# Attention values accumulated in the spare columns of the transposes' PSUM banks

## The chip, the cores and the metric

The kernel runs on one NeuronCore of a Trainium2 chip, as one launch. The metric is the device time of that launch in microseconds (us). Every execution computes the same outputs from the same inputs; before the change, three timed executions have a median of 949.86 us, between 949.14 and 950.73.

## The reference, cut to what matters

One encoder layer is applied to two sequences, a prompt of 256 tokens and a sample of 2048 tokens (2304 in all), of width 1024, in float32:

```
h = rms_norm(x, g_pre);  proj = h @ w_in            # 1024 -> 6 x 512
q, k, v, z_a, u_f, z_f = split(proj)
y_a = neighbourhood_attention(q, k, v, rpb)          # 8 heads of 64
y_f = fourier_mix(u_f) @ w_f + b_f
mixed = concat(rms_norm(y_a, g_na) * silu(z_a), rms_norm(y_f, g_f) * silu(z_f))
out = x + rms_norm(mixed @ w_out, g_post)
```

The tokens lie on a grid 64 columns wide (4 rows for the prompt, 32 for the sample). A query attends to 8 rows by 16 columns around it. The reference works on blocks of 16 query columns against a slab of 32 key columns, with a bias and a mask, a softmax, and a product with the values.

## The kernel before, in words

The projections and the Fourier half come first. The change lies in the third stage, which the code writes from line 1358 on: the attention itself, interleaved with the output projection of the Fourier half.

**Groups and steps.** The attention is cut into 36 groups: 4 pairs of heads (pr) by 9 groups. Group 0 of a pair (R is None) is the prompt; the other eight are 4 pairs of row blocks (R) by 2 halves of the columns (hc). Each group has two column blocks, b = 0 and 1, and two heads, h = 0 and 1. The loop at line 1554 runs k from 2 to 37; in step k it finishes group k-2 (called f) and starts group k (called g). The order of instructions on each engine is the order of the code (a manual schedule).

**One step, in the order of TensorE.** transp (line 1467) transposes the softmax weights of f, in pieces of 64 queries, into four PSUM banks ptb[0] to ptb[3]: block b and half y go to ptb[2b+y], alternating between y = 0 and y = 1. A bank holds 512 float32 columns; the transposes fill at most 384 of them. Each bank is then copied to SBUF (pt): the y = 0 banks by ScalarE (ACT), the y = 1 banks by VectorE (DVE), but in odd steps (the argument called short) block 1's y = 1 bank by ACT too. scores (line 1157) computes q times k of group g into four other banks. In even steps f_mm (line 1431) follows, twice: the projection of one tile of 128 tokens of the Fourier half, 12 matmuls into ptb[0] and 12 into ptb[1], each 512 columns wide, which f_evac (line 1441) scales into SBUF, the first by DVE, the second by ACT. Last comes pv (line 1485): the transposed weights times the values, for both blocks into one PSUM tile of 2 x 128 columns. That tile takes a bank of tag "c" in even steps and one of tag "a" in odd steps, the tags from which scores takes its banks.

**Gating.** The tile pv is read twice: DVE multiplies it with the gate za into y (line 1513), and ACT squares it (line 1515 for the first pair of heads, line 1519 for the others) for the later norm; GpSimd (POOL) adds the squares up (line 1520). y goes to HBM by SyncE's queue (lines 1524 and 1527). For the prompt's groups the multiplication, and the first pair's square, are split by block; for the others one instruction covers 256 columns.

**The other work of a step.** DVE adds the bias and takes the maximum for each of four score tiles (bias_max, line 1190), ACT exponentiates (exps, line 1202), DVE and POOL normalise (soft, line 1206). In even steps POOL, ACT and DVE also prepare the next tile of the Fourier half (lines 1396 to 1416). The last loop (line 1715) projects the attention half and uses ptb[0] and ptb[1] for a copy of g_post (line 1733).

**PSUM.** Of eight banks four are ptb[0] to ptb[3], three have tag "a", one tag "c". Waits between engines are generated by the framework from the order of the code and from which tiles an instruction reads or writes.

Of the kernel before, what the change touches and what calls it, by code (L numbers as in the profile page):

```python
# [10 lines left out]
F32 = mybir.dt.float32  # L11
F32R = mybir.dt.float32r
AF = mybir.ActivationFunctionType
ALU = mybir.AluOpType
# [165 lines left out]
def build(tc, A, O):  # L180
    nc = tc.nc
# [1176 lines left out]
    pt = ExitStack()  # L1358
# [59 lines left out]
    def out_mm(d, n, js, p, w):  # L1418
        for j in js:
            c, x = divmod(j, 3)  # L1420
            nc.tensor.matmul(p, (d["l"] if x == 2 else d["h"])[:, c], w(n, int(x == 1), c), start=j == 0, stop=j == 11)  # L1421
# [7 lines left out]
        nc.sync.dma_start(d["xt"], A["xn"][d["t"] * 128:d["t"] * 128 + 128, :])  # L1429

    def f_mm(d, n):
        d["p", n] = ptb[n]
        out_mm(d, n, range(12), ptb[n], lambda n, x, c: wo1[n][c][:, x])

    def a_mm(d, n):
        x = n or d is atiles[0]
# [27 lines left out]
        n = len(ds)  # L1464
        rsq_ops(inva[:, ds[0]["i"]:ds[0]["i"] + n], p[:, :n], n, 1.0 / 512)

    def transp(g, short):
        g["pt"] = []
        for b, ch in enumerate(g["ch"]):
            m = len(ch)  # L1470
            z = ch[0][0][1]
            o = jp.tile([128, 2, 384], F32, tag="pt", name="pt", bufs=PB)
            for j, c in enumerate(ch):
                for h in range(2):
                    for y, (c0, nk) in enumerate(c):
                        ys, x = slice(64 * y, 64 * y + 64), 64 * (h * m + j)
                        nc.tensor.transpose(ptb[2 * b + y][:nk, x:x + 64], g["w"][b][ys, h, c0:c0 + nk], ident[ys, ys])  # L1477
            ov = o.rearrange("p h (j y x) -> p y h j x", y=2, x=64)
            for y, copy in ((0, nc.scalar.copy), (1, nc.scalar.copy if b and short else V.tensor_copy)):
                copy(ov[:z, y, :, :m], ptb[2 * b + y][:z, :128 * m].rearrange("p (h j x) -> p h j x", h=2, x=64))  # L1480
            g["pt"].append(o)

    yt = {}

    def pv(g, short):
        pr, R = g["pr"], g["R"]
        p = ps.tile([128, 2, 128], F32, tag="a" if short else "c", name="pv", bufs=3 if short else 1)
        for b, pp in enumerate(g["pp"]):
            for j, y, nk, v, x, first, last in pp:
                o = slice(0, 128) if y is None else slice(64 * y, 64 * y + 64)  # L1490
                for h in range(2):
                    hs = slice(64 * h, 64 * h + 64)
                    nc.tensor.matmul(p[hs, b, o], v[:nk, b, x, hs], g["pt"][b][:nk, h, j * 128 + o.start:j * 128 + o.stop],  # L1493
                                     start=first, stop=last)
        ts = g["ts"]
        if R is None:
            hc = 0
            za = g["za"].rearrange("p (b r x c) -> p b x r c", b=2, x=2, c=16)
            view = lambda a: a.rearrange("p (r b x c) -> p b x r c", b=2, x=2, c=16)
            cut = lambda a: a.rearrange("p b (x r c) -> p b x r c", x=2, c=16)  # L1500
            cuts = lambda a: [a[:, b] for b in range(2)]
        else:
            cuts = lambda a: [a]
            hc = g["hc"]
            za = g["za"].rearrange("p (r b c) -> p b r c", b=2, c=16)
            view = lambda a: a.rearrange("p (r x b c) -> p x b r c", x=2, b=2, c=16)[:, hc]
            cut = lambda a: a.rearrange("p b (r c) -> p b r c", c=16)
        p4 = cut(p)
        both = lambda f, *a: [f(*x) for x in zip(*(cuts(y) for y in a))]
        if hc == 0:  # L1510
            yt[0] = jp.tile([128, 512], F32, tag="y", name="y", bufs=YB)
        y = yt[0][:, :ts.stop - ts.start]
        both(lambda o, i, z: V.tensor_tensor(out=o, in0=i, in1=z, op=ALU.mult), view(y), p4, za)
        if pr == 0:
            both(lambda o, i: nc.scalar.activation(o, i, AF.Square), view(ysq[:, ts]), p4)
        else:
            sq = jp.tile([128, 256], F32, tag="sqa", name="sqa", bufs=2)
            s4 = cut(sq.rearrange("p (b x) -> p b x", b=2))
            nc.scalar.activation(sq, p.rearrange("p b x -> p (b x)"), AF.Square)
            both(lambda o, i: nc.gpsimd.tensor_tensor(out=o, in0=o, in1=i, op=ALU.add), view(ysq[:, ts]), s4)  # L1520
        if R is None or hc:
            if R == 0:
                for x, r in enumerate(HALF[0]):
                    nc.sync.dma_start(yD[0, pr, :, TP + 64 * r:TP + 64 * r + 256], y[:, 256 * x:256 * x + 256])
            else:
                t0 = 0 if R is None else TP + 64 * HALF[R][0]
                nc.sync.dma_start(yD[0, pr, :, t0:t0 + y.shape[1]], y)
# [26 lines left out]
    for k in range(2, len(G) + 2):  # L1554
        pr, i = divmod(k, 9)
        g, p, f = G[k] if k < len(G) else None, G[k - 1] if k <= len(G) else None, G[k - 2]
        if pr < 3:
            if i == 3:
                load_k(pr + 1)
            if i == 5:  # L1560
                load_t(pr + 1, 0)
        if 0 < pr < 4 and i == 0:
            load_t(pr, 1)
        if k == 9:
            nc.sync.dma_start(gpb, pbc(A["gpost"]))
        if k == 23:
            wp = pt.enter_context(tc.tile_pool(name="wp", bufs=1, side="right"))
            WO.extend(wp.tile([128, 4, D], F32R, name="w0%d" % x) for x in range(2))
        if 24 <= k < 32:
            y = k - 24  # L1570
            nc.sync.dma_start(WO[y % 2][:, y // 2].bitcast(F32), woD[0, y % 2, y // 2])
        x = k // 2
        transp(f, k % 2)
        if k % 2:
            if g:
                scores(g)
                for b in range(2):
                    for h in range(2):
                        bias_max(g, b, h)
                        if b == 0:  # L1580
                            exps(g, b, h)
            else:
                a_mm(atiles[0], 1)
        else:
            if k > 2:
                soft(p, 0)
                exps(p, 1, 0)
                exps(p, 1, 1)
            if g:
                scores(g)  # L1590
                bias_max(g, 0, 0)
                exps(g, 0, 0)
                bias_max(g, 0, 1)
                exps(g, 0, 1)
                soft(p, 1)
                for h in range(2):
                    bias_max(g, 1, h)
                    exps(g, 1, h)
                if x < 17:
                    ys_mul(ftiles[x + 1])  # L1600
                if x < 16:
                    ys_load(ftiles[x + 2])
                f_mm(ftiles[x], 0)
            else:
                soft(p, 1)
                a_mm(atiles[0], 0)
            if k in NT:
                f_norm(NT[k])
            if k in (32, 34, 36):
                a_norm(atiles[{32: slice(6), 34: slice(6, 10), 36: slice(10, 14)}[k]])  # L1610
            if g:
                f_mm(ftiles[x], 1)
                soft(g, 0)
            run_later()
            if g:
                f_evac(ftiles[x], 0)
                soft(g, 1)
            for v, x0, x1 in YSQ.get(k, []):
                nc.scalar.activation(v[:, x0:x1], v[:, x0:x1], AF.Square)
                V.tensor_tensor(out=sqs[:, x0:x1], in0=sqs[:, x0:x1], in1=v[:, x0:x1], op=ALU.add)  # L1620
            if x < 17:
                ys_split(ftiles[x + 1])
            elif x == 17:
                ys_split(atiles[0])
            if g:
                f_evac(ftiles[x], 1)
        if pr < 3 and i == 7:
            mask_p(pr + 1)
        pv(f, k % 2)
        if k == 12:  # L1630
            pq_.close()
        if k + 1 < len(G):
            prep_v(G[k + 1])
        if k + 4 < len(G):
            prep(G[k + 4])
        if k == 28:
            xk = [kp.tile([128, T], F32, tag=x, name="xk", bufs=n) for x, n in (("kh", 2), ("kl", 1))]
        if 32 <= k < 36:
            x, d = k - 32, atiles[k - 32]
            d["xt"] = xk[x // 2][:, x % 2 * D:x % 2 * D + D]  # L1640
            nc.sync.dma_start(d["xt"], A["xn"][d["t"] * 128:d["t"] * 128 + 128, :])
        if k == 32:
            ys_load(atiles[0])
        if k in (34, 35):
            ys_load(atiles[k - 33])
            of_load(atiles[k - 34])
        if k == 36:
            ys_split(atiles[1])
# [114 lines left out]
```

## Time and profile before

| | |
|---|---|
| median of three timed executions | 949.86 us (949.14 to 950.73) |
| the profiled execution's own time | 948.03 us |
| its span, first to last instruction | 946.2 us |
| TensorE (PE) busy | 932.9 us, 99% of the span |
| DVE / ACT / POOL busy | 662.3 / 472.7 / 338.4 us |
| granted TensorE clock | 0.999 of full speed |
| the third stage, 617 to 846 us | PE 225.34, DVE 139.68, ACT 144.29, POOL 119.66 us busy of 229 |

PE is the row of matmuls and PEld that of the weight loads, which overlap matmuls. A row of the timeline gives the start in us, the duration, the engine, the line of the kernel, the operation, output and inputs, and how many were merged; brackets give how long the engine sat idle before it, and what ended that wait. In a list of waits, the three numbers are us in total, how often, and the longest.

### The profile page before, as it was taken

The page shows a single profiled execution, that of the slowest core. Times are in us where ns is not written, and L with a number is a line of the kernel's source. Part 1 is how long each engine was busy: PE and PEld are TensorE (multiplying, and loading weights), DVE is VectorE, ACT ScalarE, POOL GpSimd, SP SyncE. Part 2 cuts the span into 40 slices and gives each one's busy share as a digit, 9 for nine tenths or more (in the row PEclk, how much of TensorE's full clock was granted, in tenths as well). Part 3 has the DMA queues.
Part 4 walks back from the last instruction along what each step waited for, and adds up shares of the span by engine and source line. Part 5 has one row for each costly group of instructions (what it writes and reads, how often), then busy time and mean ns, then how long its engine had stood idle before and what let it go on. Part 6 is the DMA issues. An engine that isn't in the chain of part 4 may idle for free.

```text
span 946.2 us, 18823 instructions
## 1 busy us (share of the span) xinstructions
PE 932.9 (99%) x6800; PEld 779.8 (82%) x6800; DVE 662.3 (70%) x1287; ACT 472.7 (50%) x1053; POOL 338.4 (36%) x338
## 2 busy tenths in 40 slices
PE   9999999999999999999999999999999999999996
PEld 7889988888888888888888897978777787888885
DVE  6387987677875976696667454677565655649997
ACT  5846676532323642333344234567665666654443
POOL 3201202435650300453343000455455665524444
PEclk9999999999999999999999999999999999999999
DMA  9899776568665998669979789688788899879993
GB/s 335 319 373 372 219 281 253 164 229 312 222 266 191 363 410 322 259 217 315 326 266 325 260 312 324 222 271 240 243 271 242 259 286 272 266 238 365 339 339 126
DMA packets 146845, 265.20 MB, mean 280 GB/s; under 512 B 21888, under 2 KB 86784, under 8 KB 143872
## 3 DMA queue, kind: packets, MB, share of 16 engines
q1 hardware_dynamic: 146608, 263.99, 80.3%
q8 instruction: 54, 0.88, 0.4%
q14 instruction: 39, 0.32, 0.1%
q10 hardware_dynamic: 144, 0.00, 0.0%
HBM read 175.40 MB, written 95.88 MB: 287 GB/s over the span
## 4 chain that ended last, share of the span: by engine, by line
PE 95%; DVE 1%; DMA 1%; issue 1%; ACT 1%; POOL 0%; SPq 0%; DVEq 0%; POOLq 0%; ACTq 0%
PE mm L176 18%; PE mm L177 18%; PE mm L175 18%; PE ptb L1421 10%; PE po L1421 10%; PE pv L1493 5%; PE s L1177 4%; PE ptb L1477 3%; PE pab L1015 2%; PE py L175 1%; PE py L177 1%; PE py L176 1%; DMA rv<-wv 0%; DMA yz<-zD 0%; PE ppq L1052 0%
## 5 line engine op out<-in xcount | busy, mean ns | idle before, releaser
L175 PE MATMUL mm<-xh,wa 128*128 128x512 f32 x448 | 174.4, 389 | 0.0
L176 PE MATMUL mm<-xl,wa 128*128 128x512 f32 x448 | 174.3, 389 | 0.0
L177 PE MATMUL mm<-xh,wa 128*128 128x512 f32 x448 | 174.3, 389 | 0.0
L175 PEld LDWEIGHTS mm<-xh,wa 128*128 128x128 f32 x448 | 84.1, 188 | 17.5
L177 PEld LDWEIGHTS mm<-xh,wa 128*128 128x128 f32 x448 | 84.1, 188 | 17.5
L176 PEld LDWEIGHTS mm<-xl,wa 128*128 128x128 f32 x448 | 84.1, 188 | 17.3
L552 POOL TENSOR_TENSOR ws<-wr 128x512 f32<-128x512 f32 x16 | 22.2, 1389 | 185.1 <-DMA wr<-wz 167.6
L1421 PE MATMUL ptb<-wo,yh 128*128 128x512 f32 x272 | 86.8, 400 | 0.0
L1211 POOL TENSOR_SCALAR w<-w,m 128x352 f32<-128x352 f32 (+4 forms) x136 | 75.1, 566 | 32.8 <-DVE m L1208 17.7
L1421 PE MATMUL po<-w,yh 128*128 128x512 f32 x280 | 86.6, 391 | 0.0
L567 DVE TENSOR_TENSOR wa<-wr,wa 128x512 fp32r<-128x512 f32 x60 | 55.2, 926 | 33.3 <-ACT wa L566 33.2
L1204 ACT ACTIVATE w<-w,m 128x352 f32<-128x352 f32 (+4 forms) x136 | 69.9, 523 | 3.0 <-DVE m L1199 2.7
L869 DVE TENSOR_TENSOR f<-u,mm 128x512 f32<-128x512 f32 x64 | 43.6, 682 | 32.9 <-PE mm L177 28.0
L176 PE MATMUL mm<-vl,xh 128*128 128x512 f32 x168 | 65.5, 390 | 0.2 <-DVE vl L498 0.2
L175 PE MATMUL mm<-vh,xh 128*128 128x512 f32 x168 | 65.4, 389 | 0.0
L177 PE MATMUL mm<-vh,xl 128*128 128x512 f32 x168 | 65.4, 389 | 0.0
L1421 PEld LDWEIGHTS ptb<-wo,yh 128*128 128x128 f32 x272 | 49.3, 188 | 14.9 <-ACT pt L1480 4.1
L1421 PEld LDWEIGHTS po<-w,yh 128*128 128x128 f32 x280 | 52.3, 188 | 10.9
L1493 PEld LDWEIGHTS pv<-pt,v 96*64 96x64 f32 (+2 forms) x1280 | 45.7, 137 | 15.3 <-ACT pt L1480 8.9
L566 ACT CAST wa<-wr 128x512 fp32r<-128x512 f32 x60 | 36.4, 618 | 41.3 <-PE mm L177 17.0
L1199 DVE CUSTOM_DVE_ANT_1 w<-s,tb 128x264 f32<-128x264 f32 (+3 forms) x124 | 50.7, 455 | 7.0 <-PE s L1177 5.8
L1421 PE MATMUL po<-w,yl 128*128 128x512 f32 x140 | 54.5, 389 | 0.0
(246 smaller groups left out, 2171.6 us busy)
## 6 DMA issues: line engine op xcount, KB each, us to landing
wr<-wz SPq DMA_DIRECT2D x48, 512.0 KB
vl<-sD SPq DMA_DIRECT2D x20, 512.0 KB
xm<-xm SPq DMA_DIRECT2D x9, 1024.0 KB
oD<-ofs SPq DMA_DIRECT2D x18, 512.0 KB
of<-oD SPq DMA_DIRECT2D x18, 512.0 KB
yr<-yD SPq DMA_DIRECT2D x34, 256.0 KB
zD<-f SPq DMA_DIRECT2D x16, 512.0 KB
woD<-wo SPq DMA_DIRECT2D x16, 512.0 KB
```

The costliest lines, as they stand in the source:

```text
L175: nc.tensor.matmul(out, lh, rh, start=first, stop=False)
L176: nc.tensor.matmul(out, lh, rl, start=False, stop=False)
L177: nc.tensor.matmul(out, ll, rh, start=False, stop=last)
L566: nc.scalar.copy(o[:, 0], src)
L567: nc.vector.tensor_tensor(out=o[:, 1], in0=src, in1=o[:, 0].bitcast(F32), op=ALU.subtract)
L869: nc.vector.tensor_tensor(out=dst(f, b), in0=src(uu[u]), in1=src(p), op=op)
L1177: nc.tensor.matmul(sp[2 * b + h][64 * y:64 * y + 64, j * w:(j + n) * w], g["q"][hs, 128 * b + 64 * y:128 * b + 64 * y + 64], kk[hs, k:k + ...
L1199: nc.vector.tensor_tensor_reduce(out=rows(g["w"][b][:, h, :n], w), in0=rows(g["s"][2 * b + h][:, :n], w), in1=tv, scale=1.0, scalar=3.0e38 ...
L1204: nc.scalar.activation(w, w, AF.Exp, bias=m[:, h:h + 1], scale=-1.0, accum_out=m[:, 2 + h:3 + h])
L1211: nc.gpsimd.tensor_scalar(w, w, m[:, 4 + h:5 + h], 1.0, ALU.mult, ALU.mult)
L1421: nc.tensor.matmul(p, (d["l"] if x == 2 else d["h"])[:, c], w(n, int(x == 1), c), start=j == 0, stop=j == 11)
L1493: nc.tensor.matmul(p[hs, b, o], v[:nk, b, x, hs], g["pt"][b][:nk, h, j * 128 + o.start:j * 128 + o.stop], start=first, stop=last)
```

## The change

The values of block b are accumulated in columns 384 to 511 of ptb[b], the bank that also takes block 0's transposes of half y = b, instead of in a tile of their own. The projection of the Fourier half goes into ptb[2] and ptb[3], except for its first tile, which is computed before these two exist. The multiplication and the square are made per block for all groups, and read the two banks. The copy that ACT took in odd steps goes to DVE, as in even steps.

```diff
     def f_mm(d, n):
-        d["p", n] = ptb[n]
-        out_mm(d, n, range(12), ptb[n], lambda n, x, c: wo1[n][c][:, x])
+        p = d["p", n] = ptb[n if d is ftiles[0] else 2 + n]
+        out_mm(d, n, range(12), p, lambda n, x, c: wo1[n][c][:, x])
...
-    def transp(g, short):
+    def transp(g):
...
-            for y, copy in ((0, nc.scalar.copy), (1, nc.scalar.copy if b and short else V.tensor_copy)):
+            for y, copy in ((0, nc.scalar.copy), (1, V.tensor_copy)):
...
-    def pv(g, short):
+    def pv(g):
         pr, R = g["pr"], g["R"]
-        p = ps.tile([128, 2, 128], F32, tag="a" if short else "c", name="pv", bufs=3 if short else 1)
+        p = [ptb[b][:, 384:512] for b in range(2)]
...
-                    nc.tensor.matmul(p[hs, b, o], v[:nk, b, x, hs], g["pt"][b][:nk, h, j * 128 + o.start:j * 128 + o.stop],
+                    nc.tensor.matmul(p[b][hs, o], v[:nk, b, x, hs], g["pt"][b][:nk, h, j * 128 + o.start:j * 128 + o.stop],
                                      start=first, stop=last)
...
+        p = [cut(a) for a in p]
...
-        both(lambda o, i, z: V.tensor_tensor(out=o, in0=i, in1=z, op=ALU.mult), view(y), p4, za)
+        for b in range(2):
+            V.tensor_tensor(out=view(y)[:, b], in0=p[b], in1=za[:, b], op=ALU.mult)
         if pr == 0:
-            both(lambda o, i: nc.scalar.activation(o, i, AF.Square), view(ysq[:, ts]), p4)
+            for b in range(2):
+                nc.scalar.activation(view(ysq[:, ts])[:, b], p[b], AF.Square)
         else:
...
-            nc.scalar.activation(sq, p.rearrange("p b x -> p (b x)"), AF.Square)
-            both(lambda o, i: nc.gpsimd.tensor_tensor(out=o, in0=o, in1=i, op=ALU.add), view(ysq[:, ts]), s4)
+            for b in range(2):
+                nc.scalar.activation(cut(sq[:, b]), p[b], AF.Square)
...
```

The additions on POOL keep their number.

More of the change, by code (lines that the diff above doesn't have):

```diff
@@ L1499, in pv @@
             view = lambda a: a.rearrange("p (r b x c) -> p b x r c", b=2, x=2, c=16)
-            cut = lambda a: a.rearrange("p b (x r c) -> p b x r c", x=2, c=16)
-            cuts = lambda a: [a[:, b] for b in range(2)]
         else:
-            cuts = lambda a: [a]
             hc = g["hc"]
@@ L1506, in pv @@
             view = lambda a: a.rearrange("p (r x b c) -> p x b r c", x=2, b=2, c=16)[:, hc]
-            cut = lambda a: a.rearrange("p b (r c) -> p b r c", c=16)
-        p4 = cut(p)
-        both = lambda f, *a: [f(*x) for x in zip(*(cuts(y) for y in a))]
+        cut = lambda a: a.rearrange("p (x r c) -> p x r c", x=2, c=16) if R is None else \
+            a.rearrange("p (r c) -> p r c", c=16)
+        p = [cut(a) for a in p]
         if hc == 0:
@@ L1512, in pv @@
         y = yt[0][:, :ts.stop - ts.start]
-        both(lambda o, i, z: V.tensor_tensor(out=o, in0=i, in1=z, op=ALU.mult), view(y), p4, za)
+        for b in range(2):
+            V.tensor_tensor(out=view(y)[:, b], in0=p[b], in1=za[:, b], op=ALU.mult)
         if pr == 0:
-            both(lambda o, i: nc.scalar.activation(o, i, AF.Square), view(ysq[:, ts]), p4)
-        else:
-            sq = jp.tile([128, 256], F32, tag="sqa", name="sqa", bufs=2)
-            s4 = cut(sq.rearrange("p (b x) -> p b x", b=2))
-            nc.scalar.activation(sq, p.rearrange("p b x -> p (b x)"), AF.Square)
-            both(lambda o, i: nc.gpsimd.tensor_tensor(out=o, in0=o, in1=i, op=ALU.add), view(ysq[:, ts]), s4)
+            for b in range(2):
+                nc.scalar.activation(view(ysq[:, ts])[:, b], p[b], AF.Square)
+        else:
+            sq = jp.tile([128, 256], F32, tag="sqa", name="sqa", bufs=2).rearrange("p (b x) -> p b x", b=2)
+            for b in range(2):
+                nc.scalar.activation(cut(sq[:, b]), p[b], AF.Square)
+            o = view(ysq[:, ts])
+            if R is None:
+                for b in range(2):
+                    nc.gpsimd.tensor_tensor(out=o[:, b], in0=o[:, b], in1=cut(sq[:, b]), op=ALU.add)
+            else:
+                nc.gpsimd.tensor_tensor(out=o, in0=o, in1=sq.rearrange("p b (r c) -> p b r c", c=16), op=ALU.add)
         if R is None or hc:
@@ L1572, in build @@
         x = k // 2
-        transp(f, k % 2)
+        transp(f)
         if k % 2:
@@ L1628, in build @@
             mask_p(pr + 1)
-        pv(f, k % 2)
+        pv(f)
         if k == 12:
```

## The prediction

> **What bounds the kernel now.** I read the page first: the busy times, then the chain that ended last. Then one stretch, 617 to 846 us, which holds all steps of the changed loop, with its granted clock.
>
> ```profile
> span 946.2 us, 18823 instructions
> PE 932.9 (99%) x6800; PEld 779.8 (82%) x6800; DVE 662.3 (70%) x1287; ACT 472.7 (50%) x1053; POOL 338.4 (36%) x338
> PE 95%; DVE 1%; DMA 1%; issue 1%; ACT 1%; POOL 0%; SPq 0%; DVEq 0%; POOLq 0%; ACTq 0%
> 617.00:846.00 229.00, 225.34 (x3252) 182.84 (x3252) 139.68 (x510) 144.29 (x458) 119.66 (x187) 1.00 0.84 256
> ```
>
> PE sets the time, in the loop too: it idles 229.00 - 225.34 = 3.7 us there, while DVE, ACT and POOL are busy for little over half. So work added to DVE or ACT costs nothing by itself, and only what makes PE wait counts. The chain in order of time shows how PE runs through the end of an even step, an odd step, and into the next:
>
> ```profile
> 750.77 1.08 PE pv L1493 x32
> 751.85 0.83 PE ptb L1477 x23
> 752.68 1.21 PE s L1177 x20
> 753.89 0.07 issue
> 753.96 1.59 PE pv L1493 x40
> 755.55 0.84 PE ptb L1477 x22
> 756.39 0.73 PE s L1177 x7
> ```
>
> The reader should see that the next step's transposes (L1477) follow the values (pv, L1493) with nothing between them. Today they write other banks than pv does. After the change the first transposes write ptb[0] and ptb[1], the two banks that hold the values which DVE and ACT have yet to read. So the question is whether a transpose may start while they read other columns of its bank. The waits that the framework has put into this program answer most of it:
>
> ```profile
> ACT sqa L1519 <- DVE y L1513: 27.5, 24, 3.3
> DVE ds L1369 <- ACT dl L1367: 19.7, 9, 2.8
> ...
> 624.82 0.69 PE L1493 MATMUL pv<-pt,v 128*64 128x64 f32 x16
> 625.80 0.54 PEld L1477 LDWEIGHTS ptb<-ident,sc 64*96 64x96 f32 x15 [0.24 <-ACT ofs L1448]
> 626.12 0.48 DVE L1513 TENSOR_TENSOR y<-pv,za 128x128 f32<-128x128 f32 x2
> 626.69 0.45 ACT L1515 ACTIVATE ysq<-pv 128x128 f32<-128x128 f32 x2 [0.94 <-DVE y L1513]
> 627.19 0.37 PEld L1177 LDWEIGHTS s<-kk,q 64*64 64x64 f32 x10 [0.15 <-ACT ysq L1515]
> ```
>
> The square (L1519) takes nothing from the product y (L1513): both only read pv. Still ACT waits for DVE. The same holds for L1369, which reads the sum that L1367 read. So two engines are kept from reading one bank together. The rows at 626 show more: the prompt's group is already gated by block. Its two products run 626.12 to 626.60; the squares start at 626.69, after the second product, though the first square reads only the columns of the first product, done by about 626.40. That is the order of a whole bank, not of columns. One such pair is all that the trace has, and no row shows a PE write that waits for a reader of other columns.
>
> A rule of the Trainium skill bears on just that: the page PSUM — Partial Sum Buffer, section "PSUM bank collisions raise a hardware error", says that two of TensorE, ScalarE and VectorE on one bank and the same 32 partitions collide even on disjoint columns, reads against reads too, and that a program has to guard by bank. It speaks against this change. By it the sum is the one below; by column order it is the second rival. No run here shows a collision; the rows above agree with the guarding.
>
> **The change part by part.** First what the wait costs, from the step at 702.88:
>
> ```profile
> 702.88 0.91 PE L1477 MATMUL ptb<-ident,w 64*128 64x64 f32 x24
> 703.00 0.42 DVE L1513 TENSOR_TENSOR y<-pv,za 128x256 f32<-128x256 f32 x1 [2.63 <-PE pv L1493]
> 703.46 0.38 ACT L1519 ACTIVATE sqa<-pv 128x256 f32<-128x256 f32 x1 [1.30 <-DVE y L1513]
> 703.59 0.56 DVE L1480 COPY pt<-ptb 128x384 f32<-128x384 f32 x1 [0.16 <-PE ptb L1477]
> 703.73 1.28 PE L1177 MATMUL s<-kk,q 64*64 64x352 f32 x24
> 704.63 0.53 DVE L1199 CUSTOM_DVE_ANT_1 w<-s,tb 128x352 f32<-128x352 f32 x1 [0.49 <-PE s L1177]
> 705.31 1.59 PE L1493 MATMUL pv<-pt,v 128*64 128x128 f32 x40 [0.31 <-DVE m L1199]
> 706.23 0.08 DVE L1199 DVE_READ_ACCUMULATOR2_ANT m<- 128x1 f32 x1
> 706.84 0.90 PE L1477 MATMUL ptb<-ident,w 64*96 64x64 f32 x24
> ...
> L1513 DVE TENSOR_TENSOR y<-pv,za x40: 276/424/425, 626.1 to 844.5; 128x256 f32<-128x256 f32 x32, 128x128 f32<-128x128 f32 x8
> L1515 ACT ACTIVATE ysq<-pv x10: 272/383/384, 626.7 to 678.9; 128x256 f32<-128x256 f32 x8, 128x128 f32<-128x128 f32 x2
> ```
>
> *The new stall at each step's start.* pv computes block 0 first, in half of its 1.59 us, so block 0's product and square run under block 1's matmuls and the first transpose, into ptb[0], goes on time. The second, into ptb[1], must wait for block 1's square, and all later PE work queues behind it. Block 1's product can start when y starts now, 703.00; a 128x128 product takes 0.276 us (the minimum in its row), so 703.28; the hand-over to ACT takes 0.04 (703.42 to 703.46); a 128x128 square 0.272: 703.59; the hand-over to PE 0.05 (the squares end at 626.69 + 0.45 = 627.14, PEld starts at 627.19): 703.64. Today that second transpose starts one pace after the first: 0.91 / 24 = 0.04, so 702.92. The stall is 0.72 us. Transposes follow pv in steps 3 to 37, 35 times: 18 odd, 17 even.
>
> *After an odd step* DVE has more ahead of the product: it takes over ACT's copy. The copies start 0.72 later than 703.59, at 704.31, and two of 0.56 end at 705.43. The four bias passes, 704.63 to 706.31 today (1.68), then end at 707.11. PE's scores end at 703.73 + 1.28 + 0.72 = 705.73, and pv ends at about 705.8 + 1.59 = 707.39. Block 0's product fits between, and block 1's is not late: again 0.72, with 0.1 to 0.2 us of margin. Without that cover the stall grows by what DVE is late; one more copy, 0.56, bounds it. Sum: 35 x 0.72 = 25.2 us. Bounds: the bare product and square, 0.55 x 35 = 19.2, and 25.2 + 17 x 0.56 = 34.7.
>
> In the first step (k = 2) DVE is late already: the product starts at 626.12, when pv has ended at 624.82 + 0.69 = 625.51. There the stall is longer by that 0.6; the 0.24 that the transposes wait there now for ACT's projection read goes, since that read moves to ptb[3]. Net +0.4.
>
> *What is removed.* In odd steps pv waits after the scores, for its bank (DVE m L1199, freed by the first bias pass) and for the three copies in a row on ACT:
>
> ```profile
> PEld pv L1493 <- ACT pt L1480: 8.9, 17, 0.7
> ...
> 707.68 0.84 ACT L1480 COPY pt<-ptb 96x384 f32<-96x384 f32 x2
> 708.88 0.74 PE L1421 MATMUL ptb<-wo,yh 128*128 128x512 f32 x2
> ```
>
> At 753.89 this costs 0.07 idle and 0.07 in a pv that starts without preloaded weights (1.59, against 1.52 in even steps); at 705.01 (where the scores of 703.73 end) 0.30 and 0.07. After the change the last copy ends at 705.43, before the scores at 705.73, and the bank is long free. So 18 x 0.14 to 18 x 0.37: 2.5 to 6.7 us. I take 0.2 each, 3.6, nearer to the low end since the whole loop's idle PE time is only 3.7 us; the 8.9 us of idle weight loads lie mostly under matmuls.
>
> *The projection* in ptb[2] waits for ACT's second copy instead of its first. At 707.68 both copies together end at 708.52, PE reaches the projection at 708.88, and all of this moves by the same 0.72: cost 0. Without that margin it would be up to one copy, 17 x 0.42 = 7.1; a gain is excluded, as PE does not idle there. The reads of ptb[2] and ptb[3] end during pv, and block 1's transposes come half a transpose group later than block 0's: 0.
>
> *Smaller pieces.* DVE gains 18 copies (18 x 0.56 = 10.1 us) and 32 split products (32 x (0.55 - 0.42) = 4.2), ACT loses as many copies and gains 35 split squares (35 x (0.54 - 0.38) = 5.6); on 139.68 and 144.29 of 229 us they hide, but for the late product bounded above. POOL's additions and SP's stores of y come later with their step, by what PE is late anyway: 0. No DMA is added.
>
> Sum: 25.2 + 0.4 - 3.6 = **+22.0 us**. The profiled execution took 948.03 (span 946.2 and 1.8 around it): 970.0. The median of the timed runs lies 1.8 above that execution, so I predict 949.86 + 22.0 = **971.9 us**.
>
> **The rivals.** *No wait, columns suffice* (other side). If transposes only wait for what overlaps columns 0 to 383, the stall never occurs and the removed wait remains as gain: -2.5 to -6.7, taken -3.6: 946.3 us. For it: DVE, ACT and PE touch disjoint columns, and only one pair of rows speaks for whole banks. Against it: those rows, and the reads kept apart. It decides from the first stall below 0.1 us.
>
> *DVE late after odd steps.* If the bias passes push block 1's product, 17 stalls grow by up to 0.56: +9.5, 981.4 us. For it: the margin is 0.1 to 0.2 us. Against it: many steps have shorter bias passes.
>
> *The clock.* PE then pauses twice in each 13 us. If the granted clock fell below 1.00 in the loop, each hundredth would cost 225.34 / 100 = 2.3 us; five hundredths 11 us on top: 983 us. Against it: 1.00 in the row above, with pauses of 0.3 us already there. The Trainium skill's page TensorE: Matmul & The Clock Gate, section "A second HAM failure mode: psum-queue depth-cycling", reports such a loss from short idle times between groups of matmuls; the clock in this trace shows none.
>
> *That the change does not do what it says* comes down to the first rival's opposite, which is my forecast: the bank moves, and the freedom it should give is taken by the order of accesses.
>
> **How the numbers follow.** Forecast 0.82, columns 0.09, DVE late 0.07, clock 0.02. The range goes with the bounds: low, 19.2 + 0.4 - 6.7 = +12.9, 962.8; high, 34.7 + 0.4 - 2.5 = +32.6, 982.5. It holds the forecast, the late DVE and part of the clock's case. About 0.2% (1.9 us) is what a measurement of this kernel can tell from no change. Faster 0.09 (columns), same 0.01, slower 0.90.
>
> **What would show it.** A row of PEld for ptb (L1477's transposes) waiting for ACT's square, some 35 times at 0.7 us, 20 to 26 us in all, and PE's idle time in the loop up by as much. In odd steps no wait of pv for pt or m. The granted clock at 1.00. Wrong would be: transposes that start right behind pv, or PEld waiting instead for DVE's copies or for y behind bias passes (the second rival), or a projection that waits for pt.

## The result, and the profile after

The changed kernel takes 973.57 us (median of 5, 972.25 to 974.75) against 949.86 (949.14 to 950.73): 1.0249 times as long, 95% interval 1.0234 to 1.0264, so 23.7 us slower. The forecast was 971.9. The profiled execution took 973.57 us, its span is 971.8.

First the page, the row of the windows view for the stretch with the loop (its end moved from 846 to 872 us; columns: window, length, busy time of PE, PEld, DVE, ACT and POOL, granted clock, DMA), and the waits of PE and of its weight loads:

```profile
span 971.8 us, 18967 instructions
PE 940.2 (97%) x6800; PEld 784.0 (81%) x6800; DVE 668.5 (69%) x1337; ACT 476.3 (49%) x1070; POOL 338.2 (35%) x338
...
617.00:872.00 255.00, 233.69 (x3260) 187.72 (x3259) 148.99 (x566) 148.88 (x477) 119.93 (x187) 1.00 0.76 233
...
PE ptb L1477 <- ACT sqa L1518: 13.4, 31, 1.2
PE ptb L1477 <- ACT ysq L1514: 5.7, 12, 1.3
...
PEld ptb L1477 <- issue: 16.5, 34, 1.3
...
PEld ptb L1477 <- ACT sqa L1518: 6.8, 19, 0.5
...
PEld ptb L1477 <- POOL w L1211: 2.7, 2, 1.5
PEld ptb L1477 <- ACT ysq L1514: 2.5, 6, 0.5
```

The transposes (L1477) wait for ACT's squares, a wait that the kernel before does not have. PE's idle time in the loop grew from 3.7 to 255.00 - 233.69 = 21.3 us, by 17.6 us, while PE executes as many matmuls as before. That is less than the 23.7 us of the whole, because part of each wait counts as busy: the transpose that goes alone at 713.89 below is drawn 0.24 us long, the 23 after it 0.90 together. The same wait shows in the weight loads as 16.5 + 6.8 + 2.7 + 2.5 = 28.5 us. More than half of that has no releaser by name ("issue"), and the 2.7 us are put down to POOL. What these loads wait with is seen in the PE row beside them: at 718.57 the matmul of such a load waits for ACT's square. Reading only the loads that name the square would miss most of it. The granted clock in the loop is 1.00.

The start of a step in the timeline, after an even step (713.86) and after the next odd one (718.53). Here and below, rows that do not bear on the point are left out:

```profile
713.47 0.28 ACT L1518 ACTIVATE sqa<-ptb 128x128 f32<-128x128 f32 x1 [0.48 <-DVE y L1511]
713.84 0.29 DVE L1511 TENSOR_TENSOR y<-ptb,za 128x128 f32<-128x128 f32 x1 [0.40 <-PE ptb L1493]
713.86 0.14 PEld L1477 LDWEIGHTS ptb<-ident,w 64*128 64x128 f32 x1 [0.21 <-issue]
713.89 0.24 PE L1477 MATMUL ptb<-ident,w 64*128 64x64 f32 x1
714.16 0.28 ACT L1518 ACTIVATE sqa<-ptb 128x128 f32<-128x128 f32 x1 [0.41 <-DVE y L1511]
714.49 0.75 PEld L1477 LDWEIGHTS ptb<-ident,w 64*96 64x96 f32 x23 [0.49 <-ACT sqa L1518]
714.49 0.90 PE L1477 MATMUL ptb<-ident,w 64*96 64x64 f32 x23 [0.35 <-ACT sqa L1518]
...
716.53 1.59 PE L1493 MATMUL ptb<-pt,v 128*64 128x128 f32 x40
717.83 0.63 DVE L1511 TENSOR_TENSOR y<-ptb,za 128x128 f32<-128x128 f32 x2
718.14 0.62 ACT L1518 ACTIVATE sqa<-ptb 128x128 f32<-128x128 f32 x2
718.53 0.12 PEld L1477 LDWEIGHTS ptb<-ident,w 64*96 64x96 f32 x1 [0.55 <-issue]
718.57 1.15 PE L1477 MATMUL ptb<-ident,w 64*96 64x64 f32 x24 [0.45 <-ACT sqa L1518]
718.82 0.75 PEld L1477 LDWEIGHTS ptb<-ident,w 64*72 64x72 f32 x23 [0.17 <-ACT sqa L1518]
```

At 713.86 exactly one transpose goes, the one into ptb[0]. The next, into ptb[1], starts at 714.49, 0.05 us after block 1's square has ended at 714.44. The transposes write columns 0 to 383, the square reads 384 to 511: the order is that of the bank (or of the tile, which fills the bank; nothing here tells these two apart). After the odd step the first transpose is later still, because block 0's product can only start at 717.83, when DVE has done its bias passes. The rows from 717.83 on show one more thing: block 1's product runs while block 0's square reads the other bank. In the kernel before, at 626 us, where both blocks lay in one bank, the first square waited for both products.

To add this up over the loop, take the start of every weight load from the trace: the time from the last load of one kind to the first of the next, and the length of each run of loads.

| us over the loop | before | after | difference |
|---|---|---|---|
| from pv to the next step's transposes, 35 times | 7.16 | 23.47 | +16.3 |
| runs of transposes | 19.79 | 32.57 | +12.8 |
| runs of scores, and from scores to pv in odd steps | 34.21 | 29.46 | -4.8 |
| runs of pv | 39.42 | 38.95 | -0.5 |
| first transpose of step 2 to that of step 37 | 221.85 | 245.67 | +23.8 |

So there are 29.1 us more of stall at the 35 starts of steps, less 5.2 us that PE no longer spends elsewhere. The span grew by 25.6, not 23.8, mainly because the profiled loop began at 618.58 instead of 617.27 us; over the ten profiles of this study it begins anywhere from 617.05 to 619.85.

### The profile page after: what moved, and what is told of

Read it like the earlier page. It is cut to its first block, busy times and chain, and to the rows that moved or that the text cites. A ratio compares the mean times of both kernels' runs of the same rounds, so it can differ in the third digit from the quotient of the medians.

```text
span 971.8 us, 18967 instructions
## 1 busy us (share of the span) xinstructions
PE 940.2 (97%) x6800; PEld 784.0 (81%) x6800; DVE 668.5 (69%) x1337; ACT 476.3 (49%) x1070; POOL 338.2 (35%) x338
## 4 chain that ended last, share of the span: by engine, by line
PE 92%; DVE 4%; ACT 2%; issue 1%; DMA 1%; DVEq 0%; SPq 0%; ACTq 0%
PE mm L176 18%; PE mm L177 18%; PE mm L175 18%; PE po L1421 10%; PE ptb L1421 10%; PE ptb L1493 4%; PE s L1177 4%; PE ptb L1477 3%; PE pab L1015 2%; PE py L175 1%; DVE y L1511 1%; PE py L177 1%; PE py L176 1%; ACT sqa L1518 1%; DVE w L1199 1%
## 5 line engine op out<-in xcount | busy, mean ns | idle before, releaser
L177 PEld LDWEIGHTS mm<-xh,wa 128*128 128x128 f32 x448 | 84.1, 188 | 17.6
L552 POOL TENSOR_TENSOR ws<-wr 128x512 f32<-128x512 f32 x16 | 21.3, 1334 | 181.3 <-DMA wr<-wz 114.7
L567 DVE TENSOR_TENSOR wa<-wr,wa 128x512 fp32r<-128x512 f32 x60 | 57.3, 961 | 30.5 <-ACT wa L566 30.5
L1480 DVE COPY pt<-ptb 96x384 f32<-96x384 f32 (+4 forms) x72 | 32.4, 490 | 33.7 <-PE ptb L1477 33.7
L1493 PEld LDWEIGHTS ptb<-pt,v 96*64 96x64 f32 (+2 forms) x1280 | 45.2, 137 | 11.6 <-issue 10.5
```

The costliest lines, as they stand in the source:

```text
L177: nc.tensor.matmul(out, ll, rh, start=False, stop=last)
L567: nc.vector.tensor_tensor(out=o[:, 1], in0=src, in1=o[:, 0].bitcast(F32), op=ALU.subtract)
L1493: nc.tensor.matmul(p[b][hs, o], v[:nk, b, x, hs], g["pt"][b][:nk, h, j * 128 + o.start:j * 128 + o.stop], start=first, stop=last)
```

## The experiments

Each ratio is to the kernel before, timed on the same chip.

**The values moved back.** They have a tile of their own again, and ACT has its third copy in odd steps again. The projection in ptb[2] and ptb[3] and the split products and squares stay.

```diff
-        p = [ptb[b][:, 384:512] for b in range(2)]
+        p = ps.tile([128, 2, 128], F32, tag="a" if short else "c", name="pv", bufs=3 if short else 1)
+        p = [p[:, b] for b in range(2)]
...
-            for y, copy in ((0, nc.scalar.copy), (1, V.tensor_copy)):
+            for y, copy in ((0, nc.scalar.copy), (1, nc.scalar.copy if b and short else V.tensor_copy)):
```

> Changed kernel, but the values go into a tile of their own again (a bank of tag c in even steps, of tag a in odd ones) and ACT takes the odd steps' extra copy again. What stays of the change: the projection in ptb[2] and ptb[3], products and squares per block. Theory (transposes wait for the readers of the values' bank): all of the stall goes, 949.9 us within 1.5. Rival (the split products and squares, or the projection's new banks, cost the time): most of the 23.7 us stay, 965 us or more.

Measured: 950.62 us, 1.0018 (1.0009 to 1.0027). All but 1.4 us of the loss is gone. The copy is not what matters, as a later run with that copy alone shows, so it goes with the place of the values. The projection's place and the split instructions are nearly free, as costed. The rest is a wait for readers too: the scores, which want the bank that held the values, wait longer for the squares, now two products and two squares instead of one of each. Weight loads of this kernel:

```profile
PEld s L1177 <- ACT sqa L1519: 1.6, 6, 0.6
PEld s L1177 <- ACT ysq L1515: 0.4, 2, 0.2
```

Before, ACT's squares held up the scores for 0.8 and 0.2 us. The runs of scores are 1.5 us longer in all.

**The values in block 1's banks.**

```diff
-        p = d["p", n] = ptb[n if d is ftiles[0] else 2 + n]
+        p = d["p", n] = ptb[n]
...
-        p = [ptb[b][:, 384:512] for b in range(2)]
+        p = [ptb[2 + b][:, 384:512] for b in range(2)]
```

> Changed kernel, but the values go into the spare columns of block 1's banks, ptb[2] and ptb[3], and the projection back into ptb[0] and ptb[1]. Same number of instructions, same durations. Theory: block 0's transposes (12 in most steps, at 0.03 us each) now run before the first one that has to wait, so each of 35 stalls shrinks by about 0.31 us on average: 11 us less, 962.5 us. Rival (DVE or ACT are too loaded, whatever the bank): no change, 973.6 us. Rival (order by columns only): no change either.

Measured: 963.74 us, 1.0154 (1.0137 to 1.0171), 9.8 us less than the changed kernel (9.2 when each is taken against the kernel before on its own chip: 14.6 us of loss instead of 23.7). The timeline of this kernel at the same kind of step:

```profile
710.50 0.49 PEld L1477 LDWEIGHTS ptb<-ident,w 64*128 64x128 f32 x13
710.62 0.29 DVE L1511 TENSOR_TENSOR y<-ptb,za 128x128 f32<-128x128 f32 x1 [0.40 <-PE ptb L1493]
710.95 0.28 ACT L1518 ACTIVATE sqa<-ptb 128x128 f32<-128x128 f32 x1 [0.41 <-DVE y L1511]
711.27 0.38 PEld L1477 LDWEIGHTS ptb<-ident,w 64*72 64x72 f32 x11 [0.29 <-ACT sqa L1518]
```

Thirteen transposes now go before the wait, 12 of block 0 and the one into ptb[2], instead of one. The wait is for the same square, and the stall at this step falls from 0.76 to 0.39 us, by about the length of the twelve transposes. The projection moved too, back to ptb[0] and ptb[1], but the run before has shown its place to be nearly free. So which bank is shared, and when PE needs it, sets the loss. DVE or ACT being too busy does not explain it.

**One reader less.** The squares are taken from y in SBUF, for the first pair of heads in the same way.

```diff
-                nc.scalar.activation(cut(sq[:, b]), p[b], AF.Square)
+                nc.scalar.activation(cut(sq[:, b]), view(y)[:, b], AF.Square)
```

> Changed kernel, but ACT squares the product y in SBUF instead of the values in PSUM, so that DVE is the bank's only reader. This leaves out the right sum of squares for the norm (the squares are of gated values); the work per engine stays. Theory: the transposes wait for the product alone, and each stall loses the square and one hand-over, 0.27 + 0.04 us of 0.76: 35 x 0.31 = 10.9 us less, 962.7 us. Rival (only DVE's lateness counts): within 1 us of 973.6.

Measured: 962.62 us, 1.0139 (1.0123 to 1.0154): 13.4 us of loss instead of 23.7. The transposes' releaser changes as the theory has it:

```profile
PE ptb L1477 <- DVE y L1511: 7.8, 27, 0.8
...
709.66 0.29 DVE L1511 TENSOR_TENSOR y<-ptb,za 128x128 f32<-128x128 f32 x1 [0.40 <-PE ptb L1493]
709.99 0.31 ACT L1518 ACTIVATE sqa<-y 128x128 f32<-128x128 f32 x1 [0.38 <-DVE y L1511]
710.00 0.76 PEld L1477 LDWEIGHTS ptb<-ident,w 64*96 64x96 f32 x23 [0.33 <-DVE y L1511]
```

PE resumes at 710.00, 0.05 us after the product's end at 709.95, when the square has only begun. ACT makes as many squares as before; only its place among the bank's readers is gone, and 10 to 11 us with it.

**ACT's third copy back.**

```diff
-            for y, copy in ((0, nc.scalar.copy), (1, V.tensor_copy)):
+            for y, copy in ((0, nc.scalar.copy), (1, nc.scalar.copy if b and short else V.tensor_copy)):
```

> Changed kernel with one edit undone: in odd steps ACT copies block 1's second half again, as before the change, so that DVE has one copy less ahead of its bias passes and the product. Theory (the stall is the product and square themselves, DVE is late only in the few steps with a short pv or extra DVE work): only the steps whose stall is over 0.76 us in the changed kernel gain, some 6 by about 0.3 us: 971.8 us, 1 to 3 us less than 973.6. Rival (DVE is late after all odd steps because of that copy): 17 x 0.3 to 0.56 us: 968.5 us or less.

Measured: 973.63 us, 1.0265 (1.0248 to 1.0282): no difference from the changed kernel. The rival falls, and my 1 to 3 us did not come either. Counted against a run of transposes that waits for nothing, 27 of the 35 stalls of the changed kernel take 0.74 to 0.78 us and eight take 0.92 to 1.50, in all 3.3 us more than 0.76 each. With the copy on ACT seven of the eight are the same within 0.01 us and one is longer. All eight follow a short pv (16 or 32 weight loads instead of 40), six of them in odd steps. The changed kernel at such a step:

```profile
687.94 0.42 DVE L1199 CUSTOM_DVE_ANT_1 w<-s,tb 128x256 f32<-128x256 f32 x1 [0.22 <-PE s L1177]
688.09 0.69 PE L1493 MATMUL ptb<-pt,v 128*64 128x64 f32 x16
689.19 0.48 DVE L1511 TENSOR_TENSOR y<-ptb,za 128x128 f32<-128x128 f32 x2
689.93 0.78 PE L1477 MATMUL ptb<-ident,w 64*96 64x64 f32 x16 [1.15 <-ACT sqa L1518]
```

DVE's first bias pass waits for the scores, not for the copy. pv ends at 688.78, the passes only at 689.19, and the products come after them in DVE's order. The other two follow the even steps 2 and 4, where DVE's work for the Fourier half stands ahead of the products: after step 2, pv ends at 626.21 + 0.69 = 626.90, and the first product starts at 627.50.

**Sharing only where something covers it.** A wish for a faster kernel: the gain in odd steps (no wait of pv) without the stall. Values of odd steps go to block 1's banks, those of even steps to the tag c bank, and in even steps the scores stand before block 1's transposes. The projection is back in ptb[0] and ptb[1], and ACT has its third copy.

```diff
+            p = [ptb[2 + b][:, 384:512] for b in range(2)]    # odd steps
+            p = ps.tile([128, 2, 128], F32, tag="c", name="pv", bufs=1)    # even steps, then cut by block
...
-        transp(f)
+        transp(f, k % 2, range(2) if k % 2 or not g else range(1))
...
                 scores(g)
+                transp(f, 0, range(1, 2))
                 bias_max(g, 0, 0)
```

> Even steps: values in their own bank of tag c as in the kernel before. Odd steps: values in the spare columns of block 1's banks, ptb[2] and ptb[3]; copies as before; projection in ptb[0] and ptb[1]. In even steps the scores are computed between block 0's and block 1's transposes, so that 1.2 us of scores cover the readers of the values. Theory: no stall at either kind of step, and the odd steps' wait of pv (4.4 us in all, from the difference of the two traces) is gone: 945.5 us, or up to 949 if each of 17 more changes between transposes and scores costs PE 0.2 us. Rival (sharing a bank costs whatever the order): 955 us or more, as half of the stalls stay.

Measured: 949.87 us, 1.0007 (0.9998 to 1.0016). The stall is gone (from pv to transposes 7.17 us over the loop, as before the change), which falsifies the rival: sharing a bank costs nothing where other work stands between. The exception bears it out: step 36 has no scores to put between, and its transposes take 1.13 us instead of 0.64. But the gain, 3.2 us less than before from scores to pv and in pv, is paid back. Each even step has one more change of kind on PE: the gaps from transposes to scores, from scores to the next kind and from transposes to the projection come to 18.2 us instead of 14.8 before (scores to pv left out). And the runs of scores are 1.7 us longer than in the changed kernel (0.6 longer than before), with the split products and squares in the tag c bank.

> As the mixed kernel (block 0's transposes, scores, block 1's transposes in even steps), but with one product and one square for both blocks in even steps, as in the kernel before, so that the tag c bank comes free earlier for the next scores. Theory: the scores' waits in odd steps (1.4 us more there than with the values in shared banks) and part of pv's go: 2 us less than the mixed kernel, so 2 us or 0.2% under the kernel before. Rival (those waits have another releaser): as the mixed kernel, no difference from the kernel before.

The edit makes one product and one square of both blocks in even steps:

```diff
+        if joint:
+            p4 = p3.rearrange("p b (r c) -> p b r c", c=16)
+            V.tensor_tensor(out=view(y), in0=p4, in1=za, op=ALU.mult)
```

Measured: 948.08 us, 0.9985 (0.9976 to 0.9993). It is the one version faster than the kernel before, by 0.15%, with no change just outside its interval. By the two ratios it gains the expected 2 us on the mixed kernel. Of that the loop of the trace shows 0.9: the runs of scores fell from 23.60 to 23.14 us and the gap from scores to pv from 8.42 to 8.19, so the mechanism is there. Where the rest comes from is not shown. In the row of the loop PE idles 229.00 - 227.82 = 1.2 us:

```profile
617.00:846.00 229.00, 227.82 (x3255) 184.71 (x3256) 139.79 (x528) 151.15 (x480) 119.81 (x187) 1.00 0.84 258
```

**All scores first in even steps**, then both blocks' transposes in one piece:

```diff
-        transp(f)
+        if k % 2 or not g:
+            transp(f, k % 2)
...
                 scores(g)
+                transp(f, 0)
                 bias_max(g, 0, 0)
```

> As the mixed kernel (even steps: values in the tag c bank, product and square joined as in the kernel before; odd steps: values in the spare columns of ptb[2] and ptb[3]; projection in ptb[0] and ptb[1]), but in even steps all scores come first and then the transposes of both blocks in one piece, so that no change between transposes and scores is added. Theory: no stall, 4.4 us gained in odd steps, and 0.1 to 0.2 us in each of 17 even steps for the projection that now waits for ACT's copy right behind the transposes: 946.5 to 948 us against 949.5 of the kernel before. Rival (the copies behind the transposes are later than that, 0.5 us in each even step): 953 us.

Measured: 952.47 us, 1.0034 (1.0021 to 1.0048), above the expected range and close to its rival. The projection now follows the transposes and waits for the copy of its bank:

```profile
710.62 0.85 ACT L1480 COPY pt<-ptb 96x384 f32<-96x384 f32 x2
711.15 0.73 PE L1421 MATMUL ptb<-wo,yh 128*128 128x512 f32 x2 [0.25 <-ACT pt L1480]
```

From the last transpose to the projection's first weight load it takes 10.66 us over 18 steps, against 3.61 in the mixed kernel: 0.4 in each, where I expected 0.1 to 0.2. The scores had hidden these copies.

> As the kernel with the scores first, but in even steps block 0's transposes go bank by bank: those of ptb[0] first, so that ACT's first copy, for which the projection waits, can start about 0.15 us earlier. Theory: the projection's wait behind the transposes, 0.36 us in most even steps there, falls to 0.1 to 0.2 us; with the odd steps' gain kept that makes 17 x 0.2 = 3.4 us less than that kernel, 1 us under the kernel before. Rival (alternating banks let two transposes run in one another's shadow, so that their pace halves without it): 17 x 0.17 us more, no gain.

The edit, made on the kernel with all scores first, sorts block 0's transposes of even steps by bank:

```diff
+            seq = [(j, c, h, y) for j, c in enumerate(ch) for h in range(2) for y in range(2)]
+            if not short and b == 0:
+                seq.sort(key=lambda q: q[3])
```

Measured: 952.44 us, 1.0027 (1.0014 to 1.0041), no better. The gap before the projection fell by 1.8 us (10.66 to 8.90), and the runs of transposes grew by 2.1 (19.97 to 22.07). Of that growth 1.8 us lie in even steps; the other 0.3 are in step 3, whose order is as it was. So both effects are there and cancel. What makes the sorted order slower is not shown: the edit ends the alternation of banks, and with it that of the two halves of partitions (ys) from which the transposes read.

## Why the prediction was right, step by step

- *Whole-bank order* was the step on which all hung, inferred from one pair of rows at 626 us. It holds: moving the values back takes the loss away, moving them to banks needed later takes 9 to 10 us of it, removing one of the readers 10 to 11. Whether the order goes by the bank or by the tile that fills it stays open.
- *The stall's size.* 0.72 forecast, 0.76 measured in 27 of 35 cases; rows show products and squares of 0.28 to 0.29 us instead of their minima 0.276 and 0.272. The forecast had the first transpose on time. It is not: block 0's square ends so late that it goes 0.15 us after its time after most even steps, later after odd ones. This adds nothing, since the second transpose waits longer anyway.
- *DVE late.* Forecast +0.4 for step 2 alone, with a rival of 9.5 us after all 17 odd steps. Measured 3.3 us in eight places. In the place of step 2 it is 0.4 net, as forecast; 2.6 us in seven other places are missing from the sum. The term was mis-sized: I read the cover off a step with a 1.59 us pv and did not check the short ones. That the added copy would be what makes DVE late is wrong.
- *What is removed.* Taken 3.6 of 2.5 to 6.7, measured 5.2: 3.7 from scores to pv in odd steps, 1.1 in runs of scores that no longer wait for the tag c bank (a term I left out), 0.5 in pv. The forecast counted 18 odd steps; only 17 have scores ahead of pv. Its 0.07 us for missing preloaded weights was a misreading: 1.52 is an even step's pv in the chain, where the overlap with the matmuls before it is left out, while in the timeline pv takes 1.59 in both kinds of step, and still does after the change. What came back is that overlap: after the change pv starts at 716.53, 0.07 before the scores end (715.32 + 1.28 = 716.60).
- *Costs of nothing*: projection and split instructions hold within 1.4 us by the run with the values moved back, and the rise there lies in waits for a tile that the changed kernel doesn't have. The copies hold by the run with ACT's third copy back.
- *Sum.* Partly luck: two errors went against each other. The stall was 3.5 us larger than 25.2 + 0.4, the gain 1.6 larger than 3.6: +23.9 over the loop by the trace, +23.7 by the medians, +22.0 forecast.
- *Rivals.* Columns (the first of the list, though one sentence calls it the second): no. The clock: 1.00 in the loop. The Trainium skill's page TensorE: Matmul & The Clock Gate, section "A second HAM failure mode: psum-queue depth-cycling", has its oscillation from frequent short idle times between groups of matmuls, without a length for them; 35 pauses of 0.7 us and more, one after some 4 and one after some 9 us of work, did not bring it about here.
- *Signs.* PE's idle time was to grow by 20 to 26 us like the waits of the loads; the loads' waits came to 28.5, of which 9.3 name the square, and the idle time grew by 17.6. The sum stands on the starts of the weight loads, not on either.

## What to carry to other kernels

Columns left over in a PSUM bank are not a free bank: in these runs the engines take turns by the bank (or by the tile that fills it), so putting a result there makes its readers a predecessor of whatever PE writes to that bank next. Look at the distance on PE between the two uses: with up to 12 transposes and some 1.2 us of scores in between, the readers were hidden; next to each other they cost 0.76 us and more, 35 times. When work is put between for that purpose, count what it hid where it stood, and what one more change from one kind of matmul to another costs.

## What the runs showed of the hardware that I had not expected

Changing from one kind of matmul to another costs time even where PE's row shows no idle time. From the last weight load of one kind to the first of the next it takes 0.20 us from transposes to scores, mostly 0.41 to 0.52 from scores to the projection and 0.54 from the projection to pv, where loads within transposes follow each other at 0.03 us and those within the projection at 0.23. Part of that lies under the last matmuls of the kind before: the matmuls themselves start 0.15, 0.25 to 0.31 and 0.32 us apart at these places, against 0.02 within transposes and 0.23 within the projection. An order with one more change in each of 17 even steps paid some 3 us for it, most of the 3.2 that it had gained. What PE does in that time is not shown.
